# A two-layer trunk on one core: TensorE's order in layer 1 written out, with the scan's pieces set between dense steps

## The chip, the cores and the metric

The kernel runs on one core of a Trainium2 chip. That core has a matrix engine (TensorE, PE in the profile, with its weight loads shown apart as PEld), three engines for elementwise work (VectorE as DVE, ScalarE as ACT, GpSimd as POOL) and a queue for transfers (SyncE, SP). Each engine works through its own list of instructions in the order in which the built program holds them, and waits on semaphores for what others have to deliver. The metric is the time of one execution in device microseconds (us); lower is better.

## The reference

The computation is one inference step of a trunk with two layers on 640 tokens of width 1024: 128 prompt tokens and 512 sample tokens. Each layer normalises its input, applies a shift and a scale that come from a conditioning vector, runs one branch, and adds the branch's output times a gate to the residual `x`. Layer 0's branch is a convolution branch. Layer 1's branch, where nearly all of this change lies, is a two-directional state-space scan:

```python
u = h @ w_in
z, xbc, dt_raw = jnp.split(u, [SSD_INNER, SSD_INNER + XBC_DIM], axis=-1)
xbc = jax.nn.silu(depthwise_conv(xbc, w_conv, b_conv))      # 5 taps
xs, bm, cm = split(xbc)                                     # 2048, 4 x 128, 4 x 128
dt = softplus(dt_raw + bias);  a_cum = cumsum(dt * a)       # in chunks of 128 tokens
y_diag  = ((C B^T) * exp(segment sums)) @ (xs * dt)         # inside a chunk
state   = state * exp(a_cum[-1]) + B^T (decay * dt * xs)    # from chunk to chunk
y_off   = C @ state * exp(a_cum)
y = y_forward + flip(y_backward) + d_skip * xs
y = rms_norm_per_group(y * silu(z)) @ w_out
```

There are 4 groups of 8 heads; each group has its own B and C and its own normalisation. The kernel also returns the final scan states of the prompt.

## The kernel before

Tokens lie along the free axis and channels on the 128 partitions. All matrix products of the two layers are made in three passes of a split format: an operand is written as a rounded high part and a low part (`h_hi`, `h_lo`; `wh`, `wl`), and high x high, high x low and low x high are summed in PSUM. `split_w` (L73) loads one 128x1024 block of weights over the SP queue, has ACT round it to `wh` (L78), and has DVE or POOL subtract to get `wl` (L80). One output tile of 128 channels by 640 tokens takes 48 such matmuls (8 k-steps, 3 passes, 2 halves of the tokens). The profile counts all dense matmuls under the helper's line, L153, and the last output products under L1011. The dense tiles share one pair of PSUM buffers (`mm`), so that the tile after next waits until ACT or DVE has emptied the first.

In layer 1 each of the four groups g needs, as dense tiles: four tiles of x (`xs`), one of B, one of C, four of the gate (`pz`), and, once the group's y is normalised, eight products with `w_out` (`o2`; `out2`, four weight blocks with two tiles each). Between the dense tiles lie small matmuls in full precision, which are called pieces below:

- `ptx` (L757): transposes that turn a convolved x or B tile into token order (`to_tokens`);
- `pst` (L805): the state that one chunk adds; its operand `xw` is made by POOL (L803), and the carried state `stn` by POOL (L819) and DVE (L820);
- `pcb` (L855): C B^T of a chunk; DVE multiplies it into the decays `gf` (L864), which come from a transfer from DRAM (issued on ACT's queue), a subtraction on POOL (L841), a selection on DVE (L842) and an exponential on ACT (L848);
- `po` (L868): y_off for each direction; DVE scales it (L870) and POOL adds it to `y` (L871); `y` starts as a POOL product (L862);
- `py` (L876): y inside the chunk, 8 heads; ACT copies it to `yt` (L878);
- `pty` (L881): transposes of `y`; DVE adds them to `yt` (L882) and multiplies the sum into the gate `zs` (L889), chunk by chunk;
- `rms` (L921, L927): the sums and the spreading of a group's normalisation, with ACT's square root (L923) and DVE's reciprocal (L924) between them.

There are five chunks per group. What sets the order of all this: the program is written as generators (`phase_x`, `phase_bc`, `phase_z`, `phase_b`, `out2`), one after the other, and `phase_b` with the whole scan of a group runs under a raised priority (`tc.high_priority(offset=AHEAD)`, AHEAD 1000). The scheduler of the framework then merges them engine by engine by its own simulated times. Three `tc.issue_after` holds keep the exponentials behind the Silu of C and the square root of the group before (so that ACT changes its tables less often), and hold one gate tile back behind the normalisation.

## Time and profile before

| | |
|---|---|
| three runs | 1164.13, 1152.19 and 1165.15 us; median 1164.13 |
| the profiled execution | 1158.88 us, of which its span is 1157.1 us |
| granted TensorE clock, mean | 0.969 |
| busy: PE, PEld, DVE, ACT, POOL | 1084.6, 987.2, 819.0, 543.3, 563.9 us |
| layer 1 begins (first `dt` product) | 567.8 us; the first dense tile after the opening products starts at 591.1 us |

PE is the engine that is nearly always busy. A busy PE, however, is not a PE at its peak: the ends of matmuls are modelled, and the granted clock falls to half in some stretches. So PE's lost time has two parts, the idle time and the share of the clock that was not granted.

### The profile page before, as it was taken

Reading aid. Unit: us, or ns where it says so; the run is one execution under the profiler, and the core shown is the slowest. Engines: PE = TensorE matmul, PEld = TensorE weight load, DVE = VectorE, ACT = ScalarE, POOL = GpSimd, SP = SyncE. Lnnn points to the kernel's source line nnn. Section 1 sums busy time; section 2 is a strip of 40 time slices with the busy share of each in tenths; the row PEclk is TensorE's granted clock in tenths of the full one; section 3 lists DMA queues with packets and bytes.
Section 4 is the critical chain, followed back from the end, with each engine's and each line's share of the span. In section 5 each row is a group of like instructions: output and inputs, shape, how many; then the busy total and the mean of one; then the engine's idle time right before and its main releaser. Section 6 shows DMA issues by size and latency. Waiting matters only on the chain.

```text
span 1157.1 us, 18924 instructions
## 1 busy us (share of the span) xinstructions
PE 1084.6 (94%) x7532; PEld 987.2 (85%) x7532; DVE 819.0 (71%) x1170; ACT 543.3 (47%) x857; POOL 563.9 (49%) x475
## 2 busy tenths in 40 slices
PE   6999999999999999999999998979999998999996
PEld 3798879788899999999889977848899888998786
DVE  2478999899899599313768588745786278845875
ACT  6534456546554456212557655444165323753331
POOL 1155787869779448000000567567610766038410
PEclk8999999999999999999999999979999998999997
DMA  9334224323222211514231633414431344223302
GB/s 363 146 119 137 93 90 134 128 92 104 92 67 66 70 46 59 174 61 137 74 94 62 153 113 114 125 50 131 126 109 56 92 142 131 74 73 110 92 1 92
DMA packets 79048, 121.21 MB, mean 105 GB/s; under 512 B 5488, under 2 KB 49008, under 8 KB 78960
## 3 DMA queue, kind: packets, MB, share of 16 engines
q1 hardware_dynamic: 36720, 99.03, 25.9%
q10 hardware_dynamic: 42240, 20.98, 6.5%
q8 instruction: 59, 0.97, 0.3%
q14 instruction: 29, 0.24, 0.1%
HBM read 115.07 MB, written 4.92 MB: 104 GB/s over the span
## 4 chain that ended last, share of the span: by engine, by line
PE 67%; DVE 11%; ACT 6%; DMA 6%; POOL 5%; issue 4%; SPq 1%; ACTq 0%; DVEq 0%; POOLq 0%
PE xs L153 6%; PE o L153 6%; PE pz L153 5%; PE C L153 2%; PE B L153 2%; PE pst L805 2%; PE po L868 2%; ACT wh L78 2%; DMA wa<-w_ada 2%; DMA gf<-acd 2%; DVE cn L519 2%; DVE cva L356 2%; DMA gb<-acd 1%; PE o L1011 1%; PE o__5390 L144 1%
## 5 line engine op out<-in xcount | busy, mean ns | idle before, releaser
L356 DVE SCALAR_TENSOR_TENSOR cva<-v,cst,cva 128x550 f32<-128x550 f32 (+12 forms) x386 | 286.3, 815 | 9.2 <-ACT cva L349 7.7
L78 ACT CAST wh<-wf 128x1024 fp32r<-128x1024 f32 (+1 forms) x128 | 127.0, 993 | 251.0 <-PE o__4921 L144 37.6
L80 POOL TENSOR_TENSOR wl<-wf,wh 128x1024 fp32r<-128x1024 f32 (+1 forms) x62 | 148.2, 2390 | 128.4 <-ACT wh L78 123.5
L80 DVE TENSOR_TENSOR wl<-wf,wh 128x1024 fp32r<-128x1024 f32 (+1 forms) x66 | 79.9, 1210 | 91.3 <-ACT wh L78 91.1
L385 POOL TENSOR_TENSOR cv<-cv,tp 128x490 f32<-128x490 f32 (+3 forms) x94 | 113.4, 1210 | 13.4 <-ACT cv L383 9.0
L153 PE MATMUL o<-yhl,wh 128*128 128x320 f32 x384 | 93.3, 326 | 0.0
L841 POOL TENSOR_TENSOR gf<-gf,cols 128x512 f32<-128x512 f32 x40 | 46.2, 1164 | 81.7 <-DVE cols L728 63.9
L803 POOL TENSOR_TENSOR xw<-xt,cols 128x512 f32<-128x512 f32 x32 | 36.1, 1139 | 97.4 <-ACT xt L758 65.5
L153 PE MATMUL pz<-h_hi,wl 128*128 128x384 f32 (+1 forms) x256 | 83.4, 326 | 0.0
L380 ACT ACTIVATE tp<-v,cst 128x490 f32<-128x490 f32 (+3 forms) x94 | 65.9, 716 | 37.4 <-POOL cv L385 37.2
L153 PE MATMUL pz<-h_hi,wh 128*128 128x384 f32 (+1 forms) x256 | 82.0, 320 | 0.2 <-ACT zs L789 0.2
L153 PE MATMUL pz<-h_lo,wh 128*128 128x384 f32 (+1 forms) x256 | 81.8, 320 | 0.0
L153 PE MATMUL xs<-h_hi,wh 128*128 128x384 f32 (+1 forms) x224 | 72.8, 325 | 0.5 <-ACT up L641 0.5
L153 PE MATMUL xs<-h_hi,wl 128*128 128x384 f32 (+1 forms) x224 | 73.1, 327 | 0.0
L841 POOL TENSOR_TENSOR gb<-gb,cols 128x512 f32<-128x512 f32 x40 | 47.6, 1196 | 51.5 <-DMA gb<-acd 37.7
L736 DVE SCALAR_TENSOR_TENSOR xs<-up,cst,xs 128x642 f32<-128x642 f32 x64 | 68.5, 1077 | 4.8 <-ACT xs L734 4.0
L153 PEld LDWEIGHTS o<-yhl,wh 128*128 128x128 f32 x384 | 65.0, 189 | 7.6 <-issue 7.4
L153 PE MATMUL xs<-h_lo,wh 128*128 128x384 f32 (+1 forms) x224 | 71.5, 319 | 0.0
L842 DVE COPY_PREDICATED gf<-msk,gb 128x512 f32<-128x512 int32 x40 | 40.3, 1020 | 38.7 <-POOL gf L841 32.1
L153 PE MATMUL o<-yhl,wl 128*128 128x320 f32 x192 | 63.5, 331 | 0.0
L630 POOL MEMSET up<- 128x2 f32 x2 | 0.2, 100 | 117.2 <-DVE h_lo L215 117.2
L871 POOL TENSOR_TENSOR y<-y,yo 128x512 f32<-128x512 f32 x32 | 46.8, 1463 | 14.2 <-DVE yo L870 13.3
(681 smaller groups left out, 3364.9 us busy)
## 6 DMA issues: line engine op xcount, KB each, us to landing
wf<-w_in SPq DMA_DIRECT2D x48, 512.0 KB, 3.5
wa<-w_ada SPq DMA_DIRECT2D x64, 256.0 KB, 5.1
wf<-w_out SPq DMA_DIRECT2D x24, 512.0 KB, 3.5
wf<-w_xbc SPq DMA_DIRECT2D x24, 512.0 KB, 3.6
gf<-acd ACTq DMA_DIRECT2D x40, 256.0 KB, 4.0
gb<-acd ACTq DMA_DIRECT2D x40, 256.0 KB, 3.4
wa<-w_ada SPq DMA_DIRECT2D x16, 512.0 KB, 9.9
wf<-w_z SPq DMA_DIRECT2D x16, 512.0 KB, 3.6
```

The source lines that it names most:

```text
L78: S.copy(out=wh[:, :n], in_=wf[:, :n])
L80: sub.tensor_sub(out=wl[:, :n], in0=wf[:, :n], in1=wh[:, :n].bitcast(F32))
L153: T.matmul(ps[:, b, at : at + t1 - t0], lhsT=w, rhs=t[:, t0:t1], start=k == 0 and n == 0, stop=k == nk - 1 and n == 2)
L356: V.scalar_tensor_tensor(out=rows(acc)[:, :, lo:hi], in0=rows(v)[:, :, lo + d : hi + d], scalar=w_dw(i, tap), in1=rows(acc)[:, :, lo:hi], ...
L380: S.activation(out=tp[:, :, 0 : hi - lo], in_=rows(v)[:, :, lo + d : hi + d], func=AF.Copy, scale=w_dw(i, tap))
L385: G.tensor_add(out=rows(out)[:, :, lo:hi], in0=rows(out)[:, :, lo:hi], in1=tp[:, :, 0 : hi - lo])
L519: then(V.tensor_sub(out=t, in0=cv[i], in1=mu))
L736: V.scalar_tensor_tensor(out=acc, in0=u[:, d : d + PW], scalar=c("w_c", j * 5 + d), in1=acc, op0=ALU.mult, op1=ALU.add)
L803: G.tensor_mul(out=D8(xw), in0=D8(xt[ch]), in1=bc64(cols2[ch], 32 * back + o8))
L841: last_sub[g] = G.tensor_sub(out=gt, in0=gt, in1=cols1[ch][:, o : o + 4].unsqueeze(2).broadcast_to([P, 4, 128]))
L842: V.copy_predicated(out=gf, mask=msk.unsqueeze(1).broadcast_to([P, 4, 128]), data=gb)
L871: G.tensor_add(out=y, in0=y, in1=yo)
```

## The change

1. **A written-out order of TensorE in layer 1.** The generators are cut finer. The dense work becomes one list, `fill`, whose steps of six matmuls (`dense_steps`) come one after the other: x(0), B(0), C(0), x(1), z(0), B(1), C(1); then for g = 1 and 2 x(g+1), the products with `w_out` of group g-1, z(g), B(g+1), C(g+1); for g = 3 z(3) and the products of group 2; then the last products. A planner, `drive`, keeps a clock that each matmul advances by a fixed amount, and between two dense steps it sets a piece as soon as the piece's planned time has come and what it needs has been set. The scan of group g gives each of its steps a distance in shares of a period (7.5, 17, 17 and 9.5 us for the four groups), transposes come 13 us after their tile, and the normalisations have distances of 3 to 6 us. At the end every PE instruction of layer 1 is tied to the one before it, so the scheduler can't change PE's order; the other engines' order is still the scheduler's, with a raised priority (AHEAD 300) for scan, normalisation and transposes.
2. **y in x's place.** ACT copies `py` over the chunk's x (`xt`), and DVE adds `pty` there. `yt` is gone.
3. **The gate follows the last chunk.** z is computed between the chunks; its product with y is made when all chunks of the group are done (8 products per half of the tokens, of 64 and 256 columns, in place of one of 512 per chunk). `yh` and `yl` are made in halves.
4. **Holds gone, queues changed.** The `issue_after` holds are gone. The saved states are loaded over ACT's queue, no longer over SP's. The `wl` of the first groups' x, B and C tiles are subtracted on POOL instead of DVE.
5. **Start of layer 0.** The first two blocks of the conditioning product get two more 128x256 products after each fourth matmul (8 in all), into a PSUM tile that is overwritten later.

The core of the diff:

```diff
+            if busy is not None and k % 4 == 3:
+                for b in range(2):
+                    T.matmul(busy[:, b, 0:256], lhsT=w[:, 0:128], rhs=w, start=True, stop=True)
...
+        def drive(filler, streams):
+            needs = next(filler, None)
+            while True:
+                streams[:] = [z for z in streams if z.alive]
+                hit = [z for z in streams if z.free() and z.due <= clock[0]]
+                if hit:
+                    hit[0].step()
+                    continue
+                hit = [i for i, p in enumerate(pending) if p[0] <= clock[0]]
+                if hit:
+                    emit_pending(hit[0])
+                    continue
+                if needs is not None and all(n in done for n in needs):
+                    needs = next(filler, None)
+                    continue
...
+                clock[0] = max(clock[0], min(due))
...
+                        T.matmul(ps[:, b, at_ : at_ + t1 - t0], lhsT=w, rhs=t_[:, t0:t1], start=k == 0 and n == 0, stop=k == nk - 1 and n == 2)
+                        clock[0] += (t1 - t0) / 2400 + 0.0135
+                    if k % 2:
+                        yield ()
...
-                nc.sync.dma_start(out=st[c0], in_=a[key][g])
+                nc.scalar.dma_start(out=st[c0], in_=a[key][g])
...
-                            hold.enter_context(tc.issue_after(grp[g]["silu"].ins))
-                            if g:
-                                hold.enter_context(tc.issue_after(last_root[g - 1].ins))
...
             for n, ch in enumerate(order):
+                gfs = grp[g]["gfs"]
+                if n < 3:
+                    chain(n, 1)
+                if n < 4:
+                    grp[g]["gfs"] = decays(g, order[n + 1])
+                elif g < 3:
+                    grp[g + 1]["gfs"] = decays(g + 1, (ORDER if g < 2 else ORDER3)[0])
+                if n:
+                    yield 0.1 * T_, ()
+                    turn_y(order[n - 1], y)
+                yield 0.1 * T_, ()
...
-                yt = lp.tile([P, 512], F32, tag="yo", bufs=2, name="yt")
-                S.copy(out=yt, in_=py)
+                S.copy(out=xt[ch], in_=py)
+                yield (0.35 if n < 4 else 0.0) * T_, ()
...
+        def norm(g, sides):
+            yield 0.0, [("y", g, ch) for ch in chs] + ([("out2", g - 1, mp) for mp in range(4)] if g else [])
+            for j in range(4):
+                yield 0.0, [("z", g, j)]
...
+                        V.tensor_mul(out=z, in0=z, in1=yv)
+            done.add(("gated", g))
...
+        drive(filler(), [Stream(scans()), Stream(norms()), Stream(final(1)), Stream(final(0))])
+        for ins in nc.cur_bb.bb.instructions[begun:]:
+            if ins.engine == mybir.EngineType.PE:
+                if prev is not None:
+                    tc.add_manual_dep(ins, prev, mybir.DependencyInfo(mybir.DependencyClass.NoSync, mybir.DependencyReason.DATA), reason="order")
+                prev = ins.name
```

Three places show what this does to the order. The first is PE at the normalisation of group 0. Before, the end of the gate tiles is followed by both halves of the sums, their spreading and five states at a stretch, with no dense step among them (`pz` is a dense step of the gate, `ptx` a transpose of B, `pst` a state):

```order
L153 MATMUL pz<-h_hi,wl 128x256
L921 MATMUL rms<-ysq,ones 32x160 x8
L757 MATMUL ptx<-cst,B 128x128
L921 MATMUL rms<-ysq,ones 32x160 x8
L927 MATMUL rms<-rq,cst 128x160 x4
L805 MATMUL pst<-xw,Bt 128x512 x5
L153 MATMUL pz<-h_hi,wh 128x384
```

Now the sums of group 0 come in four parts among the x tiles of group 2; after the first of them stand 18 dense matmuls, of which the first three are shown, then the second part:

```order
L809 MATMUL xs<-h_hi,wl 128x384
L1067 MATMUL rms<-ysq,ones 32x160 x4
L809 MATMUL xs<-h_hi,wh 128x384
L809 MATMUL xs<-h_lo,wh 128x384
L809 MATMUL xs<-h_hi,wl 128x384
```

The sums, the spreading and the states have each moved apart, with 6 to 24 dense matmuls between two of them.

The second place is PE at the end of group 3, from the last dense step of group 2's products with `w_out` (`o_10740`) to the first of the last products (`o_10913`), as it stands now:

```order
L809 MATMUL o_10740<-yhl,wl 128x320
L1067 MATMUL rms<-ysq,ones 32x160 x2
L972 MATMUL pty<-cst,y 128x128 x4
L991 MATMUL pcb<-C,B 128x128
L1007 MATMUL po<-st_f_10071,C 128x512
L1067 MATMUL rms<-ysq,ones 32x160 x2
L1007 MATMUL po<-stn,C 128x512
L1022 MATMUL py<-gf,xt 64x128 x8
L1067 MATMUL rms<-ysq,ones 32x160 x4
L972 MATMUL pty<-cst,y 128x128 x4
L1077 MATMUL rms<-rq,cst 128x160 x2
L1152 MATMUL o_10913<-yhl,wh 128x320 x2
```

Between the last `o_10740` and the first `o_10913` no dense step is left: the whole last chunk and the normalisation of the second half of the tokens lie there. Before, the last chunk's pieces began among dense steps of the same products (`o_10410`):

```order
L855 MATMUL pcb<-C,B 128x128
L153 MATMUL o_10410<-yhl,wh 128x320 x2
L868 MATMUL po<-st_f_10464,C 128x512
L153 MATMUL o_10410<-yhl,wl 128x320
L153 MATMUL o_10410<-yhl,wh 128x320 x2
L153 MATMUL o_10410<-yhl,wl 128x320
L153 MATMUL o_10410<-yhl,wh 128x320 x2
L927 MATMUL rms<-rq,cst 128x160 x2
L153 MATMUL o_10410<-yhl,wl 128x320
L153 MATMUL o_10410<-yhl,wh 128x320
L868 MATMUL po<-stn,C 128x512
```

They went on so through the next tile (`py` behind 14 of its matmuls), and that chunk's `pty` stood 47 matmuls into the last products. The dense work that used to cover the last chunk has been moved ahead of it.

The third place is ACT in the scan of group 0, now, around the exponentials of a chunk's decays (`gf`), with Silu of an x tile before them (`up` is where the next dense tile is emptied to, `wh` the rounded weights):

```order
L827 ACT_TABLE_LOAD
L827 ACTIVATE xs<-xs 128x642
L916 ACT_TABLE_LOAD
L916 ACTIVATE gf<-gf 128x512
L911 DMA gb<-acd 128x4x128
L78 CAST wh<-wf 128x1024
L916 ACTIVATE gf<-gf 128x512
L911 DMA gb<-acd 128x4x128
L638 COPY up_5967<-xs 128x128
L639 COPY up_5967<-xs 128x512
```

Before, in the scan of group 1, the exponentials of two chunks followed on one load (`yt` is the copy of `py`):

```order
L848 ACT_TABLE_LOAD
L848 ACTIVATE gf<-gf 128x512
L840 DMA gb<-acd 128x4x128
L78 CAST wh<-wf 128x1024
L848 ACTIVATE gf<-gf 128x512
L840 DMA gb<-acd 128x4x128
L840 DMA gf<-acd 128x4x128
L878 COPY yt<-py 128x512
L840 DMA gf<-acd 128x4x128
L78 CAST wh<-wf 128x1024
L848 ACTIVATE gf<-gf 128x512
```

Silu of the x tiles, which changes the table, has come between the exponentials. In layer 1 the list of ACT held 33 table loads before (13 at the exponentials, 10 at the convolved tiles, 6 at the gate, 4 at the square roots); it now holds 44 (18, 11, 11 and 4).

499 lines of the change are left out of this document (305 added, 194 removed).

## Prediction

> **What bounds the kernel now.** I read the page first: of 1157.1 us PE is idle for 72.5, no other engine is busy for more than 71%.
>
> ```profile
> span 1157.1 us, 18924 instructions
> PE 1084.6 (94%) x7532; PEld 987.2 (85%) x7532; DVE 819.0 (71%) x1170; ACT 543.3 (47%) x857; POOL 563.9 (49%) x475
> ```
>
> The change sits in layer 1, so next I cut that layer into stages (the view of windows; columns: stage, its length, busy us of PE, PEld, DVE, ACT, POOL, then the granted clock and the transfers). The stages are: the opening and group 0's scan; group 0's normalisation and group 1's scan; the dense stretch and group 2's scan; its normalisation with the dense tiles behind it; group 3's scan; the end.
>
> ```profile
> 590.00:735.00 145.00, 134.73 (x873) 122.98 (x871) 113.43 (x146) 83.90 (x130) 67.45 (x51) 0.98 0.38 112
> 735.00:835.00 100.00, 89.36 (x563) 74.32 (x563) 63.60 (x97) 37.65 (x57) 66.25 (x51) 0.93 0.36 108
> 835.00:960.00 125.00, 123.75 (x844) 112.67 (x843) 79.15 (x117) 55.51 (x90) 54.45 (x45) 1.00 0.34 103
> 960.00:1030.00 70.00, 66.90 (x481) 65.05 (x480) 53.53 (x64) 39.00 (x65) 21.28 (x16) 0.95 0.31 92
> 1030.00:1100.00 70.00, 68.26 (x431) 56.31 (x430) 43.09 (x71) 24.39 (x41) 44.70 (x35) 0.98 0.30 91
> 1100.00:1157.00 57.00, 45.51 (x290) 41.21 (x289) 37.68 (x88) 14.65 (x33) 3.62 (x3) 0.86 0.13 47
> ```
>
> What PE loses in a stage is its idle time plus the clock not granted (length times one minus the clock). In order that is 10.3+2.9, 10.6+7.0, 1.3+0, 3.1+3.5, 1.7+1.4 and 11.5+8.0 us: 13.2, 17.6, 1.3, 6.6, 3.1 and 19.5, together 61.3. An order can win nothing else in layer 1, since the number of its matmuls does not change. The 41.8 us before 1100 are the ceiling for the pieces; the end has its own reasons.
>
> Then who PE waits for (the view of waits, PE alone, from 590 us on; us in total, times, longest):
>
> ```profile
> PE pty L881 <- POOL y L871: 5.3, 3, 2.6
> PE pst L805 <- POOL xw L803: 5.3, 4, 3.5
> PE pty L881 <- POOL y L862: 3.9, 2, 3.1
> PE ptx L757 <- ACT xs L737: 3.1, 1, 3.1
> PE rms L927 <- DVE rq L924: 2.6, 1, 2.6
> ...
> PE xs L153 <- ACT up L641: 0.5, 1, 0.5
> ```
>
> All are pieces that stood in PE's list before their operand was made; no dense tile waits for its weights, and only one for a buffer, 0.5 us. The second stage shows how such waits come on top of one another (windows again):
>
> ```profile
> 755.00:760.00 5.00, 2.64 (x9) 2.63 (x10) 2.32 (x4) 4.58 (x7) 4.74 (x4) 0.50 0.34 105
> 760.00:765.00 5.00, 3.76 (x6) 0.92 (x4) 5.00 (x10) 2.60 (x4) 2.78 (x2) 0.81 0.00 0
> 765.00:770.00 5.00, 2.19 (x4) 0.80 (x4) 2.11 (x4) 1.46 (x2) 5.00 (x5) 0.87 0.01 2
> 770.00:775.00 5.00, 4.78 (x14) 3.77 (x13) 0.62 (x1) 2.31 (x6) 2.42 (x3) 0.50 0.27 102
> ```
>
> Here PE runs only 33 matmuls in 20 us, is idle for 6.6, and the clock is at half for the first and last five.
>
> **The change part by part.** Prices of a dense tile of 48 and of two pieces (the chain in order of time: start, us, what):
>
> ```profile
> 777.10 0.86 PE pst L805 x2
> 783.79 1.02 PE py L876 x16
> 1002.64 7.03 PE B L153 x48
> ```
>
> So a dense matmul costs 0.147 us, and a state 0.86.
>
> *Group 0's normalisation and group 1's start.* Their pieces now stand among x tiles with 6 to 24 dense matmuls, 0.9 to 3.5 us, between two. The chain sums, root, reciprocal, spreading has 24 dense matmuls and two states (5.2 us) between sums and spreading; the wait for `rq` was 2.6 us with nothing between, so it is covered. The states waited up to 3.5 us for `xw`; now 12 or more dense matmuls lie between them. Of 17.6 us I leave 5: DVE also convolves x tiles here, and half of the longest waits may remain. Gain 12.6 (bounds 5 and 17.6).
>
> *Group 2's normalisation* is the same move with smaller waits: of 6.6 I leave 3, a gain of 3.6 (bounds 0 and 6.6).
>
> *Group 0's scan.* Here POOL must be weighed against PE, for z and x(1) are now all that fills it. POOL's operations (the view of groups from 590 us on: count, busy us, mean ns, then its idle time):
>
> ```profile
> L841 POOL TENSOR_TENSOR gb<-gb,cols 128x512 f32<-128x512 f32 x40 | 47.6, 1196 | 51.5 <-DMA gb<-acd 37.7 <-DVE gf L864 7.1 <-DVE xs L736 6.6
> L871 POOL TENSOR_TENSOR y<-y,yo 128x512 f32<-128x512 f32 x32 | 46.8, 1463 | 14.2 <-DVE yo L870 13.3
> L841 POOL TENSOR_TENSOR gf<-gf,cols 128x512 f32<-128x512 f32 x40 | 46.2, 1164 | 81.7 <-DVE cols L728 63.9 <-DMA gf<-acd 12.8 <-DVE C L736 2.3
> L803 POOL TENSOR_TENSOR xw<-xt,cols 128x512 f32<-128x512 f32 x32 | 36.1, 1139 | 97.4 <-ACT xt L758 65.5 <-PE pst L805 31.8
> L862 POOL TENSOR_TENSOR y<-xt,co 128x512 f32<-128x512 f32 x20 | 26.3, 1315 | 11.0 <-DVE wl L999 9.5 <-DVE co L860 1.5
> L819 POOL TENSOR_TENSOR stn<-stn,decb 128x512 f32<-128x512 f32 x16 | 19.8, 1237 | 5.4 <-DVE stn L820 5.4
> ```
>
> A chunk costs POOL two `gf` and two `gb` (4.7), `y` (1.3) and two additions (2.9): 9.0; a state step adds 2.4 (`xw`, `stn`), a final prompt state 1.1. That is 12.5 for the first two chunks, 11.3 for the third, 9.0 for the fourth. By the new order PE has, from one `pty` to the next, 60 dense matmuls and pieces (14.5 us), 54 (11.3), 24 (7.0) and 72 (12.3). POOL is ahead at first, level at the second gap, and 2 us late at the third; PE waits there, and at the first `xw`, which needs four subtractions and itself (5.9 us) after the columns, where PE has 24 dense matmuls (3.5): 2.4. The wait for `ptx` (3.1) stays, since that piece stands no later than before, and some 2.5 for `py` where DVE still selects decays ahead of it. Sum 10 of 13.2, a gain of 3. Bounds: the whole 13.2, or a loss of 12 if POOL keeps the pace of before (first rival).
>
> *The end of the dense list.* Nothing dense covers group 3's last chunk any more. After the last `o_10740` the chain is: C B^T, DVE's work on it, POOL's `y` and two additions (1.3+2.9), DVE's share between, transposes, and beside it root, table load, reciprocal, spreading and the first `yh`: by these prices and the delays in group 0 about 12 us, with 6 us of pieces to run. PE idles for some 6; this is new. Loss 6.5 with a slice of the clock (bounds 2 and 12).
>
> *The last stage* keeps its shape: the second half's products wait for sums and root, and a final stretch of output and transfers.
>
> ```profile
> 1124.00:1128.00 4.00, 4.00 (x13) 3.10 (x14) 2.98 (x8) 2.20 (x6) 0.00 (x0) 0.50 0.00 0
> 1128.00:1132.00 4.00, 2.81 (x10) 2.41 (x10) 4.00 (x11) 0.00 (x0) 0.00 (x0) 0.50 0.70 246
> ```
>
> Between 1124 and 1132 the first half's six scalings on DVE stand before the second half's normalisation; the planner spaces them out. I count 4 (bounds 0 and 8).
>
> *Start of layer 0.* The clock there is at half while transfers run at their full rate:
>
> ```profile
> 20.00:22.00 2.00, 1.24 (x12) 0.67 (x12) 0.86 (x2) 1.32 (x2) 0.67 (x1) 0.79 1.03 409
> 22.00:24.00 2.00, 2.00 (x15) 1.53 (x7) 0.00 (x0) 0.00 (x0) 1.69 (x1) 0.50 1.04 411
> 30.00:32.00 2.00, 2.00 (x14) 1.19 (x14) 2.00 (x2) 0.64 (x1) 1.56 (x1) 0.65 1.04 414
> ```
>
> Half clock from 21 to 31 us costs 5. The eight extra products lie in front of this stretch, where PE is idle, and can keep the clock up; but transfers feed PE there, and the new order sets a matmul of the third tile sooner than its weights come. I take a gain of 2 (bounds 5, and a loss of 2 if the extra products delay the first normalisation). The Trainium skill, "TensorE: Matmul & The Clock Gate", Part 1, says that the clock returns to full after about 3.4 us of activity; by it the whole 5 would be won, and the sum be 3 lower.
>
> *Costs beside the path.* DVE's 8 smaller gate products, the halves of `yl` and ACT's halves of `yh` add about 2 us each per engine and lie on engines that are busy for 390 and 255 of 567 us. Moving 8 `wl` from DVE to POOL falls before the scan, where POOL is idle. The saved states' loads leave SP's queue, which frees weights behind them, and no dense tile waited for weights. ACT gets 11 more table loads (the view of groups):
>
> ```profile
> L848 ACT ACTIVATE gf<-gf 128x512 f32<-128x512 f32 x40 | 24.3, 628 | 49.5 <-DVE gf L842 47.8 <-DMA gb<-acd 1.6
> L848 ACT ACT_TABLE_LOAD x13 | 16.7, 1283 | 0.2
> ```
>
> At 1.283 us that is 14.1 us on an engine that has 312 free; I count nothing, but it is the root of the third rival.
>
> **The sum.** 12.6 + 3.6 + 3 - 6.5 + 4 + 2 = 18.7 us less than the profiled execution's own 1158.88: 1140. That execution lies 5.2 under the median of the runs shown (1164.13) and 6.7 over the fastest (1152.19), so a median may come out some 5 us to either side.
>
> **The rivals.** *First: nothing is won, since the scan has a pace of its own.* Transposes of `y` before, four of group 0 and the first two of group 1 (PE in order of time):
>
> ```profile
> 686.13 0.60 PE L881 MATMUL pty<-cst,y 128*128 128x128 f32 x4
> 702.63 0.66 PE L881 MATMUL pty<-cst,y 128*128 128x128 f32 x4 [2.64 <-POOL y L871]
> 719.10 0.65 PE L881 MATMUL pty<-cst,y 128*128 128x128 f32 x4 [1.86 <-POOL y L871]
> 730.83 0.66 PE L881 MATMUL pty<-cst,y 128*128 128x128 f32 x4
> ...
> 788.16 0.60 PE L881 MATMUL pty<-cst,y 128*128 128x128 f32 x4
> 802.86 0.60 PE L881 MATMUL pty<-cst,y 128*128 128x128 f32 x4
> ```
>
> Those of group 0 came 16.5, 16.5 and 11.7 us apart. If that is what transfer, POOL, DVE and ACT need in a row for a chunk, not what the old order left them, PE waits 2.0, 5.2 and 4.7 us against the new 14.5, 11.3 and 7.0: 12 us in group 0. Group 3, which is planned nearly as tight, would add 6. The gain of 18.7 falls to 1: 1158, between 1150 and 1168. For it: POOL's 37.7 us of idle time on `gb` transfers, which the sum of busy times leaves out. Against it: group 1's first chunk took 14.7 us with the same work.
>
> *Second: the pieces are never late.* Then of the 41.8 us only the wait for `ptx` stays (3.1), the gap at the end shrinks to 2, and with 4 and 2 from the ends the gain is 42: 1117, between 1108 and 1128. For it: from 835 to 960, where dense steps and pieces were already mixed, PE lost 1.3 in 125 us. Against it: POOL's count for group 0.
>
> *Third: slower, because ACT is held.* The exponentials now stand on ACT among the copies that empty the dense tiles (`up`) and the roundings of weights (`wh`). An exponential waits for DVE's selection: 49.5 us over 20 chunks, 2.4 each. With a load to its table and one back, a chunk holds ACT for 5 us. PE has one buffer in reserve, a dense tile of 7.03 us, so the hold is hidden as long as it stays under that. It decides as soon as DVE comes to the selection late by four of the convolution's operations (some 4 us): then PE waits 2.3 to 3 us per chunk, 46 to 60 us over 20 chunks. From 1140 that is 1186 to 1200, with half of the chunks some 1168. For it: the holds that kept exponentials behind Silu are gone. Against it: no dense tile waited before for more than 0.5 us on ACT, though ACT then waited 47.8 us at the same place. The Trainium skill, "ScalarE: Activation LUTs", What ACT_TABLE_LOAD costs and the section on table sets, speaks against this change: it gives 1.28 us for the load and as much again for a drain, 2.66 us a switch, and says to finish with one set before going to the next. The row agrees on the load, and no row here shows the drain; by it the hold would be an estimated 7.7 us and this rival would decide without DVE's being late.
>
> **How the numbers follow.** The forecast has a chance of 0.50, with a range of its own from 1128 to 1150; the first rival 0.17, the second 0.22, the third 0.11. A measurement of this kernel can tell about 2% from no change; on the profiled execution's time that line is at 1136. A bit under half of the forecast's chance (0.22) and the second rival lie below it: faster 0.44. The rest of the forecast (0.28) and the first rival lie within: 0.45. Slower: 0.11. The range of 1113 to 1170 leaves out the lower part of the second rival (0.06) and nearly all of the third.
>
> **What the changed profile would show.** Right: in the stage of group 0's normalisation PE's idle time falls from 10.6 to a few us, and the clock there goes from 0.93 to about 1; the waits for `rq` and `xw` all but go; a gap of 4 to 8 us appears ahead of the first of the last products, after which the clock dips; `pty` of group 0 comes 12 to 15 us apart at first. First rival: long waits of `pty` for `y` in groups 0 and 3. Second: less than 5 us of waits before that gap. Third: dense tiles that wait for ACT's `up` or `zs`. The forecast is wrong if the gap at the end costs over 12 us, if the first state waits long for columns that come later than before, or if layer 0 moves by more than 5 us, which I have not looked for beyond its first 60.

## The result, and the profile after

The changed kernel takes 1201.51 us (median, 1199.82 to 1205.28) where the kernel before takes 1158.16 (1150.32 to 1165.15): a ratio of 1.038, with a 95% interval from 1.029 to 1.047. It is slower; the forecast was 1140. The page of the changed kernel, its span and its busy times:

```profile
span 1198.0 us, 19044 instructions
PE 1090.4 (91%) x7548; PEld 988.6 (83%) x7548; DVE 844.6 (71%) x1218; ACT 561.7 (47%) x880; POOL 589.0 (49%) x483
```

Apart from the extra products at the start PE does the same work, and it is idle for 107.6 us instead of 72.5. Nearly all of the difference lies in layer 1, which I count from the first matmul of `dt` (PE in order of time, the kernel before and the changed one):

```profile
567.80 0.90 PE L144 MATMUL dt<-h_hi,wh 128*128 128x384 f32 x2 [0.55 <-ACT h_hi L210]
```

```profile
565.63 0.56 PE L148 MATMUL dt<-h_hi,wh 128*128 128x384 f32 x2 [0.55 <-ACT h_hi L214]
```

From there to the end of the span is 589.3 us before and 632.4 after: 43.1 more. To see where, I cut both kernels at the same events: first dense tile, first state of group 0, then the last `py` of group 0, 1, 2 and 3, and the end. (Windows; columns as in the prediction: stage, length, busy us of PE, PEld, DVE, ACT, POOL, granted clock, transfers.) Before:

```profile
590.80:657.10 66.30, 62.35 (x421) 61.47 (x421) 52.03 (x71) 43.26 (x69) 10.04 (x9) 0.97 0.40 111
657.10:738.50 81.40, 75.33 (x475) 64.59 (x475) 64.53 (x81) 40.77 (x61) 58.66 (x45) 0.98 0.38 116
738.50:837.60 99.10, 88.10 (x551) 72.90 (x551) 62.70 (x97) 37.78 (x57) 66.63 (x52) 0.93 0.36 107
837.60:973.60 136.00, 135.11 (x928) 123.73 (x928) 86.61 (x127) 58.72 (x95) 62.05 (x51) 1.00 0.35 105
973.60:1101.10 127.50, 122.65 (x819) 109.26 (x818) 87.65 (x122) 60.10 (x99) 56.74 (x44) 0.96 0.28 87
1101.10:1157.10 56.00, 44.41 (x283) 40.30 (x282) 36.58 (x86) 13.68 (x31) 3.62 (x3) 0.85 0.14 48
```

The changed kernel, at the same events:

```profile
588.60:657.50 68.90, 55.02 (x349) 53.20 (x349) 60.41 (x68) 40.19 (x65) 32.55 (x17) 0.94 0.36 103
657.50:739.20 81.70, 70.89 (x425) 59.77 (x426) 56.05 (x78) 38.77 (x56) 56.90 (x44) 0.92 0.37 109
739.20:884.70 145.50, 134.84 (x886) 120.79 (x885) 95.28 (x135) 65.61 (x102) 69.69 (x53) 0.96 0.31 93
884.70:1027.20 142.50, 133.59 (x880) 118.88 (x879) 92.50 (x138) 66.34 (x102) 66.03 (x51) 0.98 0.32 97
1027.20:1132.90 105.70, 97.39 (x652) 83.31 (x652) 71.33 (x123) 45.57 (x72) 53.51 (x42) 0.98 0.30 90
1132.90:1198.00 65.10, 46.32 (x280) 40.97 (x280) 37.26 (x89) 16.76 (x37) 3.03 (x3) 0.80 0.12 41
```

The lengths of a stage cannot be compared, since the dense work in it differs. What can be compared is the loss as the prediction counts it, idle time plus length times one minus the clock:

| stage | loss before | loss after | difference |
|---|---|---|---|
| opening, to the first state | 5.9 | 18.0 | +12.1 |
| scan of group 0 | 7.7 | 17.3 | +9.6 |
| normalisation of group 0, scan of group 1 | 17.9 | 16.5 | -1.4 |
| normalisation of group 1, scan of group 2 | 0.9 | 11.8 | +10.9 |
| normalisation of group 2, scan of group 3 | 10.0 | 10.4 | +0.4 |
| from group 3's last `py` to the end | 20.0 | 31.8 | +11.8 |

The sum of the differences is 43.4, the whole of the 43.1. Four rows stand out: the opening, group 0's scan, the stretch around group 1's normalisation, which had lost almost nothing before, and the end. A single stage, however, moves from one execution to the next: the run without the extra products (under "The other two parts"), whose layer 1 is written the same, takes 634.0 us for it and loses 21.8, 16.2, 11.5, 11.2, 14.0 and 32.1 us in these six stages. Differences of up to 5 us in one stage are therefore no evidence by themselves.

PE's waits in the changed kernel, first from 588 to 740 us (us in total, times, longest):

```profile
PE ptx L846 <- ACT xt L848: 8.6, 5, 3.7
PE pty L972 <- POOL y L1011: 6.6, 1, 6.6
PE pst L940 <- POOL xw L938: 5.6, 1, 5.6
...
PE xs L809 <- POOL wl L80: 1.2, 1, 1.2
```

From 740 to 1133, and from 1133 to the end:

```profile
PE rms L1067 <- ACT ysq L1059: 11.4, 6, 3.2
PE o L809 <- DVE x L168: 3.5, 2, 2.6
```

```profile
PE o L1152 <- ACT yhl L1086: 4.4, 2, 2.7
PE o L1152 <- DVE yhl L1087: 2.2, 2, 1.6
```

Added up over all of layer 1, the waits that this view labels are 65.8 us; in the kernel before they are 32.2. They are called labelled waits below. The waits for `rq` and most of those for `xw` in the normalisations went, as forecast, and waits of the sums (`rms`) for the squares took their place: before, these had been 2.2 us in all. At the end, the second half waits for its normalised rows. DVE there (in order of time), the kernel before and the changed one:

```profile
1125.32 1.92 DVE L932 SCALAR_TENSOR_TENSOR zs<-zs,cst,rms 128x320 f32<-128x320 f32 x4 [0.77 <-PE rms L927]
1127.16 0.48 DVE L934 TENSOR_TENSOR yhl<-zs,yhl 128x320 fp32r<-128x320 f32 x1
1127.56 2.83 DVE L1031 SCALAR_TENSOR_TENSOR fo<-x,cst,rps 128x320 f32<-128x320 f32 x6
```

```profile
1165.18 2.84 DVE L1190 SCALAR_TENSOR_TENSOR fo<-x,cst,rps 128x320 f32<-128x320 f32 x6 [1.20 <-PE rps L182]
1167.94 1.92 DVE L1085 SCALAR_TENSOR_TENSOR zs<-zs,cst,rms 128x320 f32<-128x320 f32 x4
```

Before, the scaling of the second half's rows (`zs`) stood ahead of the six output scalings of the first half (`fo`). Now the six stand ahead of it: PE spreads the normalisation (`rms`) only from 1164.94 us on, after the products that the output scalings wait for.

### The profile page after: what moved, and what is told of

Its sections match the earlier page's. It is cut to its first block, busy times and chain, and to the rows that moved or that the text cites. A ratio compares the mean times of both kernels' runs of the same rounds, so it can differ in the third digit from the quotient of the medians.

```text
span 1198.0 us, 19044 instructions
## 1 busy us (share of the span) xinstructions
PE 1090.4 (91%) x7548; PEld 988.6 (83%) x7548; DVE 844.6 (71%) x1218; ACT 561.7 (47%) x880; POOL 589.0 (49%) x483
## 5 line engine op out<-in xcount | busy, mean ns | idle before, releaser
L80 POOL TENSOR_TENSOR wl<-wf,wh 128x1024 fp32r<-128x1024 f32 (+1 forms) x70 | 170.0, 2430 | 160.9 <-ACT wh L78 148.6
L80 DVE TENSOR_TENSOR wl<-wf,wh 128x1024 fp32r<-128x1024 f32 (+1 forms) x58 | 73.0, 1259 | 94.8 <-ACT wh L78 94.6
L826 DVE SCALAR_TENSOR_TENSOR xs<-up,cst,xs 128x642 f32<-128x642 f32 x64 | 83.5, 1310 | 12.8 <-ACT xs L824 12.2
L809 PE MATMUL pz<-h_hi,wh 128*128 128x384 f32 (+1 forms) x256 | 89.4, 349 | 0.0
L809 PE MATMUL xs<-h_hi,wh 128*128 128x384 f32 (+1 forms) x224 | 81.2, 363 | 0.5 <-ACT up L639 0.5
L913 DVE COPY_PREDICATED gf<-msk,gb 128x512 f32<-128x512 int32 x40 | 42.8, 1094 | 54.1 <-POOL gf L912 52.7
L809 PE MATMUL pz<-h_hi,wl 128*128 128x384 f32 (+1 forms) x256 | 79.6, 311 | 0.0
L809 PE MATMUL o<-yhl,wl 128*128 128x320 f32 x192 | 59.7, 311 | 0.0
L938 POOL TENSOR_TENSOR xw<-xt,cols 128x512 f32<-128x512 f32 x32 | 39.6, 1240 | 40.7 <-PE rms L1067 33.4
L809 PEld LDWEIGHTS pz<-h_hi,wh 128*128 128x128 f32 x256 | 48.9, 191 | 7.0 <-issue 7.0
```

Of the source, the lines that this page charges most:

```text
L80: sub.tensor_sub(out=wl[:, :n], in0=wf[:, :n], in1=wh[:, :n].bitcast(F32))
L809: T.matmul(ps[:, b, at_ : at_ + t1 - t0], lhsT=w, rhs=t_[:, t0:t1], start=k == 0 and n == 0, stop=k == nk - 1 and n == 2)
L826: V.scalar_tensor_tensor(out=acc, in0=u[:, d : d + PW], scalar=c("w_c", j * 5 + d), in1=acc, op0=ALU.mult, op1=ALU.add)
L913: V.copy_predicated(out=gf, mask=msk.unsqueeze(1).broadcast_to([P, 4, 128]), data=gb)
L938: G.tensor_mul(out=D8(xw), in0=D8(xt[ch]), in1=bc64(cols2[ch], 32 * back + o8))
```

## The experiments

Layer 0 is the same code in nearly all these kernels, and yet layer 1 began anywhere from 564.6 to 572.8 us. So beside the time each verdict gives the length of layer 1, from the first `dt` to the end of the span, against 632.4 of the changed kernel and 589.3 of the kernel before. These are mostly single profiled executions; I take nothing under about 4 us for a difference.

### The tie of TensorE's order

```diff
-        for ins in nc.cur_bb.bb.instructions[begun:]:
-            if ins.engine == mybir.EngineType.PE:
-                if prev is not None:
...
-                prev = ins.name
```

> The changed kernel without the last loop, which ties each TensorE instruction of layer 1 to the one before it; everything is still emitted in the planned sequence, but the scheduler sets TensorE's order. Theory A (the written order sets pieces ahead of operands that come later than the plan's delays; 33 us more of labelled waits, and about 10 us of clock behind them): the waits fall back towards 32 us and the time to 1160-1175. Theory B (ACT is held by the exponentials' table loads, so that copies come late whatever the order): 1190-1205, with the same waits for ACT.

Measured: 1177.0 us, layer 1 605.2, so 27.2 of the 43.1 come back. By the same six events the losses are 11.7, 16.4, 10.1, 10.6, 8.7 and 15.2, together 72.7 against 62.4 in the kernel before; so 5.6 of the 15.9 us that layer 1 is still longer stand in no stage's loss, but in PE's busy time. The last stage, where it shows most (windows):

```profile
1115.30:1175.20 59.90, 49.48 (x337) 45.21 (x336) 41.13 (x97) 18.95 (x40) 1.15 (x1) 0.92 0.16 53
```

Its loss of 15.2 stands against 31.8; the opening gains 6.3 and group 0's normalisation 6.4. The scan of group 0 still loses 16.4 and the opening 11.7, so these parts have a cause beside the tie. Theory A (the written order puts pieces where their operands are not ready) holds for the larger part of the loss; labelled waits fell to 48 us only, not to 32.

### The exponentials on ACT

```diff
-            for gf in gfs:
-                S.activation(out=gf, in_=gf, func=AF.Exp)
```

> The changed kernel without the 40 exponentials of the decays (the decays are left as the selected differences, so the scan's result is another one). It takes 25 us of exponentials and about 20 table loads, 25 us, off ACT. Theory B (ACT held): waits for xt, xs, ysq, up and yhl, 31 us of the 65, fall by more than half and the time to 1165-1180. Theory A (the plan's delays): the time stays within 1188-1203, since only the py waits for gf (2.2 us) and a share of the xt waits go.

The kernel leaves out the exponentials, so its result is another one. Measured: 1195.4, layer 1 626.8: 5.6 us less. The table loads of layer 1 fall from 47 to 12 and ACT loses 25 us of exponentials, and yet the long waits remain (`pty` for `y` 6.7, `pst` for `xw` 3.5, `ptx` for the convolved tiles). Theory B, my third rival, falls: what ACT holds is hidden nearly everywhere.

### The pace of group 0, and POOL's list

```diff
-            for g, T_ in enumerate((7.5, 17.0, 17.0, 9.5)):
+            for g, T_ in enumerate((10.0, 17.0, 17.0, 9.5)):
```

> The changed kernel with the pace of group 0's scan set from 7.5 to 10. Theory A: between two transposes of y lie some 40% more dense matmuls, the 6.6 us wait for y in group 0 goes, the first wait for xw (5.6) and the ptx waits (9) stay: 1188-1194. Theory C (POOL's list in a row has its own pace, about 15 us a chunk): the same gain here, 5 to 9 us. If instead the lost time is only moved on, to the dense tiles that wait for group 0's normalisation, it stays at 1196-1203.

Measured: 1206.1, layer 1 636.4: 4.0 more. The wait of 6.6 for `y` became 1.3 and 3.8, one of 2.7 for `gf` and one of 4.9 for `xt` came, and the dense list ran out, so that group 0's third to fifth `py` stand after 98 to 102 us of dense matmuls, nearly on top of one another. Both theories had this wrong; only the alternative that the lost time is moved on is left standing.

```diff
                 if n < 3:
                     chain(n, 1)
-                if n < 4:
-                    grp[g]["gfs"] = decays(g, order[n + 1])
...
+                if n < 4:
+                    grp[g]["gfs"] = decays(g, order[n + 1])
                 if n == 4:
                     done.add(("scan", g))
```

> The changed kernel with the decays of the next chunk emitted after this chunk's y and its two additions instead of ahead of them, so that POOL's subtractions on gb, which wait for transfers (43.9 us of POOL's idle time), no longer stand before y. Theory C: the 6.6 us wait of pty for y in group 0 goes and those at the end (1.5 and 1.0) fall: 1186-1193. Theory A without C: the decays only come later, py waits for gf instead (more than the 2.2 us it has now): 1198-1215.

Measured: 1209.6, layer 1 635.0: 2.6 more, and `pty` still waits 5.9 for `y`. POOL's subtractions ahead of `y` were not what held it; theory C falls.

### The stock of dense work beside group 0

```diff
+        def bc_tile(g):
+            us = []
+            for name in ("B", "C"):
...
+                yield from dense_steps(ps, wh, wl, h, [k * 128 for k in range(KD)], ODD)
+                us.append(evacuate(ps))
...
+            if g:
+                yield (("scan", g - 1),)
```

> The changed kernel in which the B and C tiles of the next group run their dense matmuls (two tiles of 7.03 us) before the plan waits for the end of the running scan, and only their convolutions wait. Theory D (group 0's scan keeps its pace in real time, and what the new order changed is the stock of dense work beside it: the last py of group 0 stands after 101 us of dense matmuls, against 119 before): that py now stands after 109, so 8 us come back, 1187-1193. Theory A (single delays of the plan are too short, the stock does not matter): the waits only move, 1196-1203.

Measured: 1200.1, layer 1 631.3. Group 0's last `py` indeed stands after 109 us of dense matmuls, but it also starts 181.6 us after the start of layer 1 instead of 173.6: eight more done, eight more taken. Theory D in this form falls. Time since the start of layer 1 less 0.147 us for each dense matmul that stands ahead in the list, the time lost by that point, is some 72.6 in both (about 51.7 in the kernel before).

### The delays before the sums, and at the end

```diff
-                yield 3.0, ()
+                yield ((7.0 if j == 0 else 4.0) if g < 3 else 3.0), ()
                 if j == 0:
                     ps[sides[0]] = spare("rms")
```

> The changed kernel with the plan's delays between the squares of a group's normalisation and their sums set from 3 to 7 for the first and to 4 for the others, in groups 0 to 2. Theory E (the gate products of a whole group now stand in a row between the last chunk and the first square, a chain that the delay of 3 does not cover): the six waits of rms for ysq in groups 0 to 2, 11.4 us, and the half clock that comes behind each go, 1184-1193. Rival: what is blocked until the normalisation is done comes later by the same, 1196-1205.

Measured: 1194.9, layer 1 622.8, 9.6 us less; layer 1 had begun 4.8 us later than in the changed kernel, which hides half of it in the time. The third and fourth stage (windows) and the wait of the sums up to 1133 us:

```profile
744.20:880.40 136.20, 131.38 (x888) 117.29 (x889) 89.53 (x135) 65.13 (x102) 73.34 (x53) 1.00 0.33 99
880.40:1018.60 138.20, 131.05 (x879) 117.69 (x879) 92.55 (x138) 68.80 (x104) 68.00 (x51) 0.99 0.34 100
```

```profile
PE rms L1067 <- ACT ysq L1059: 3.2, 4, 1.2
```

The same matmuls take 9.3 and 4.3 us less there, idle time and clock alike: losses of 4.8 and 8.5 against 16.5 and 11.8, and the waits are 3.2 instead of 11.4. Theory E holds: a delay of 3 was too short for sixteen gate products and a square. Of the 13.6 us in these two stages 9.6 are left in layer 1, since the opening and the end lose more than in the changed kernel.

```diff
-                yield 3.0, ()
+                yield (3.0 if g < 3 else 1.5), ()
...
-                yield (6.0 if b == sides[0] else 4.0), ()
+                yield ((6.0 if g < 3 else 3.0) if b == sides[0] else 4.0), ()
```

> The changed kernel with the plan's delays of group 3's two normalisations halved (3 to 1.5 between squares and sums, 6 to 3 before the spreading). Theory F (the second half's normalisation is spread over the whole of the first half's products by these delays, so that its scaling falls behind the first half's six output scalings on DVE): the waits for yhl at the second half, 2.7 and 1.6 us, and the half clock behind go, 1191-1195. Rival: the sums wait for the squares on the spot and nothing is won, 1197-1203.

Measured: 1197.6, layer 1 629.1, which no single execution tells from no change. The stage from group 3's last `py` to the end is 59.6 us and not 65.1, and it loses 25.1 instead of 31.8; 4.7 of this gain is clock. DVE has the scaling of the second half's rows ahead of the six output scalings again, as before the change, and yet the waits for `yhl` are 5.6 instead of 6.6: they were not what shortened it, so the mechanism that I gave is not shown.

The three edits in one kernel:

> The edits of the three runs before in one kernel. If they are separate causes the gains add: 8 + 10 + 6, 1174-1182. If they are one slack that is spent once, it is no better than the best of them, 1185-1193.

Measured: 1188.3, layer 1 615.4: 17.0 us less, a little over the sum of the single gains (1.1 + 9.6 + 3.3). The expectation missed since it had 8 for the early tiles.

### Where the opening loses

```diff
-                later(42.0 + n, lambda n=n, z=z: turn_columns(n, z))
-            later(49.0, lambda: None, ("cols",))
+                later(50.0 + n, lambda n=n, z=z: turn_columns(n, z))
+            later(59.0, lambda: None, ("cols",))
```

> The changed kernel with the pieces that turn the time steps' columns set 8 and their readiness 10 later in the plan, so that the first state of group 0 stands after 70 us of dense matmuls (as before) and not after 60; but the dense work that may run beside group 0's scan ends as before the edit, so its last py still stands after 101 (119 before). Read from the start of layer 1, to leave layer 0 out. Theory D (what counts is how much dense work may stand beside the scan until its end): the first state comes with no wait, and the time lost is only moved to the later chunks, within 3 us of the changed kernel. Theory A (a piece set too early is the loss by itself): the 5.6 us for xw and part of the ptx waits are won, 6 to 10 us less.

Measured: 1200.8, layer 1 634.3: no difference. The first state came 11.3 us later, with 9.7 us more dense matmuls ahead of it. So it is not pinned to a time at which its operand is ready: counted in the same way, PE loses some 32 to 34 us up to it wherever it stands (about 19 in the kernel before). So it is not this delay alone; something else slows the opening too.

All edits together, and transposes of x tiles later:

```diff
-        TURN = 13.0
+        TURN = 16.0
...
-            later(TURN + 2.0, lambda: part(0, 1), key)
+            later(TURN + 5.0, lambda: part(0, 1), key)
```

> All at once: columns later, B and C dense tiles early, longer delays before the sums in groups 0 to 2, shorter ones in group 3, and the transposes of x tiles 3 later (13 to 16, the second 5 behind the first instead of 2). The last py of group 0 now stands after 113 us of dense matmuls. Theory D: group 0's scan ends at the same real time with 12 us more work done, 10 us less than the kernel with three edits (1188.3), so 1174-1181. If the scan is only pushed out by what stands beside it, as with the B and C edit alone: 1185-1192.

Measured: 1197.2, layer 1 624.4, worse than three of its edits. Where these 9.0 us went is not shown: the opening loses about as much as with the three edits (18.8 and 18.2), and the scan and the normalisation of group 0 and the end lose more. But one new wait in the opening points to DVE (waits of PE, 594 to 673 us):

```profile
PE ptx L846 <- ACT xs L827: 8.7, 1, 8.7
```

The transposes now wait for the convolved tile itself, which ACT finishes from DVE's steps. Two parts of the change load DVE there. The four x tiles of group 1 stand where z tiles stood, and each brings four convolution steps; and the eight subtractions `wl` that went to POOL run beside DVE's work. DVE's convolution steps and one small operation in the opening, the kernel before and the changed one (groups; count, busy us, mean ns):

```profile
L736 DVE SCALAR_TENSOR_TENSOR xs<-up,cst,xs 128x642 f32<-128x642 f32 x16 | 13.8, 883 | 2.8 <-ACT xs L734 2.8
...
L682 DVE SCALAR_TENSOR_TENSOR e<-xr 128x384 f32<-128x384 f32 x1 | 0.6, 561 | 0.0
```

```profile
L826 DVE SCALAR_TENSOR_TENSOR xs<-up,cst,xs 128x642 f32<-128x642 f32 x22 | 27.2, 1253 | 2.5 <-ACT xs L824 2.4
...
L680 DVE SCALAR_TENSOR_TENSOR e<-xr 128x384 f32<-128x384 f32 x1 | 2.5, 2518 | 0.0
```

More of them, and each longer. Why that one operation takes 2.52 us shows beside POOL (both engines of the changed kernel in order of time):

```profile
588.37 4.71 POOL L80 TENSOR_TENSOR wl<-wf,wh 128x1024 fp32r<-128x1024 f32 x2 [7.41 <-ACT wh L78]
```

```profile
590.98 2.52 DVE L680 SCALAR_TENSOR_TENSOR e<-xr 128x384 f32<-128x384 f32 x1
```

POOL's second subtraction ends at 593.08; DVE's operation, 0.56 us long when alone, ends at 593.50. It has been held until POOL was done. The twenty-two convolution steps are not all longer by the same: sixteen last 0.87 to 0.92 us, as before, three that run while POOL makes a `wl` last 2.9 to 3.0, and three later ones, beside POOL's work on the decays and on `xw`, about 1.5. Each of the two parts was undone by itself:

```diff
-            item(x_tile(0, j), a["w_xbc"][j] if j > 1 else None, G)
+            item(x_tile(0, j), a["w_xbc"][j] if j > 1 else None)
...
-            item(x_tile(1, j), a["w_xbc"][4 + j], G)
+            item(x_tile(1, j), a["w_xbc"][4 + j])
```

> The changed kernel with the eight subtractions wl of the first tiles back on DVE. Theory H (each of POOL's 2.4 us subtractions holds the DVE operation that runs beside it: 0.88 us for a convolution step alone, 1.63 beside POOL): DVE gains more in the opening than its own subtractions (1.3 us each) cost, the first state comes 2 to 6 us sooner after the start of layer 1 (91.9 now), and layer 1 is 2 to 6 us shorter than 632.4. Rival (moving them off DVE is worth its own time): DVE carries 9 us more in the opening and the first state comes 3 to 9 us later.

Measured: 1196.3, layer 1 629.3, 3.1 less. The convolution steps are back at 969 ns, but DVE's own nine subtractions take 12.2 us there, and the first state comes at 93.0 us instead of 91.9. The two nearly cancel. The opening (windows) loses 20.8 us where it lost 18.0:

```profile
588.20:658.20 70.00, 56.21 (x349) 54.38 (x349) 57.92 (x76) 41.39 (x66) 11.78 (x9) 0.90 0.34 102
```

```diff
-        for j in range(4):
-            item(x_tile(1, j), a["w_xbc"][4 + j], G)
         for g in range(NG):
...
             for j in range(4):
                 item(z_tile(g, j), a["w_z"][4 * g + j])
+            if g == 0:
+                for j in range(4):
+                    item(x_tile(1, j), a["w_xbc"][4 + j], G)
```

> The changed kernel with the four z tiles of group 0 set ahead of the four x tiles of group 1 in the dense list, as before. Theory G (x tiles in the opening bring four convolution steps each to DVE, which is busy for 85 to 92% there, so that the transposes and the first state wait): the waits up to the first state fall from 13.5 us to 5 or less, and the first state comes 6 to 10 us sooner; as the stock beside the scan is no larger, up to half of it is lost again by the scan's end: layer 1 is 5 to 10 us shorter than 632.4. If DVE is not what holds it: no change, 628-636.

Measured: 1200.7, layer 1 628.7, 3.7 less; the first state came 1.1 us sooner only. By itself this is not enough either, and the opening loses 17.7 us:

```profile
593.20:661.00 67.80, 55.56 (x349) 53.57 (x349) 50.96 (x65) 37.90 (x62) 19.68 (x13) 0.92 0.33 97
```

To see POOL's subtractions alone, the kernel before was given that one part:

```diff
-            wh, wl = split_w(src, 1024, V)
+            nin[0] += 1
+            wh, wl = split_w(src, 1024, G if nin[0] <= 8 else V)
```

> The kernel before with one part of the change alone: the wl subtractions of its first eight tiles of layer 1 that are split there (x 2 and 3, B, C, z) on POOL. Theory H: each holds the DVE operation beside it, convolution steps there last over 1.2 us and not 0.88, and the first state comes 2 to 6 us later than 89.3 us after the start of layer 1. Rival (DVE is relieved by 8 x 1.3 us and POOL was idle): 0 to 5 us sooner.

Measured: 1174.5, layer 1 602.9 against 589.3: 13.6 us longer. Its opening (windows), its convolution steps there (groups) and the waits of PE there:

```profile
592.80:663.30 70.50, 59.39 (x376) 58.03 (x377) 55.15 (x63) 42.24 (x65) 34.12 (x19) 0.93 0.36 103
```

```profile
L739 DVE SCALAR_TENSOR_TENSOR xs<-up,cst,xs 128x642 f32<-128x642 f32 x16 | 22.2, 1405 | 0.0
```

```profile
PE pt L727 <- DVE t L718: 3.5, 1, 3.5
PE ptx L760 <- ACT xs L740: 2.8, 1, 2.8
PE pt L727 <- DVE v L714: 2.6, 1, 2.6
PE xs L153 <- POOL wl L80: 1.2, 1, 1.2
```

The same sixteen steps take 22.2 us instead of 13.8: twelve last at most 0.88 us and four, beside a `wl` on POOL, 2.99 to 3.03. The time steps' columns, which are a chain on DVE, come late, and the opening loses 16.0 us instead of 5.9. Theory H holds there. DVE is rid of nine of its ten subtractions in this stage and is yet busy for 55.2 us and not 52.0: moving them to the idle engine gives the busy one no relief, and what is held stands in the chain to the first state. Some of the 13.6 lies further on (a z tile waits 6.4 us for ACT), which I have not followed up.

### All together, with and without the tie

The written order kept, with z before x(1), `wl` on DVE, early B and C tiles, later columns and the changed delays (edits as above):

> The written order kept, with z before x(1), the wl subtractions on DVE, B and C dense tiles early, columns 8 to 10 later, and the changed delays of the sums. The first state stands after 70 us of dense matmuls and group 0's last py after 113. If theories D, G and H hold together, group 0 ends with some 55 us lost and not 72.6 (51.7 before), and layer 1 takes 595-608: 1163-1176. If the written order costs by itself whatever its numbers, 612 or more.

Measured: 1182.8, layer 1 614.7: the opening is right, the whole is not. Its first stage (windows) and its longest waits:

```profile
589.30:656.20 66.90, 62.87 (x422) 61.33 (x422) 52.29 (x71) 39.81 (x66) 10.75 (x9) 0.97 0.38 113
```

```profile
PE ptx L846 <- ACT B L827: 11.7, 1, 11.7
PE py L1026 <- DVE gf L1005: 9.3, 4, 5.7
PE pst L944 <- POOL xw L942: 8.9, 5, 5.5
```

The opening loses 6.0 us, as the kernel before does (5.9), and by group 0's last `py` 56.4 us are lost, where 55 were expected. So it took these parts together to bring the opening back; none of them undone alone did, and how they share the loss is not shown. Then one piece alone, the transposes of group 1's B, stands 11.7 us too early, and the stage in which it lies loses 27.7 us where the changed kernel lost 16.5. New waits came for those that went: the nine tied kernels with an edited plan took back 17.7 us at most and stayed between 614.7 and 636.4.

The same without the late columns and without the tie:

> The same without the late columns and without the tie of TensorE's instructions. Without the tie alone layer 1 took 605.2, all of its 16 us over the kernel before in group 0. Theory G and H: these 16 fall to 5 or less, layer 1 takes 588-596, 1156-1165, the time of the kernel before. If group 0's loss has another cause: 600-606.

Measured: 1166.3, layer 1 599.0: 33.4 of the 43.1 are back. 9.7 remain, where 5 or less were expected. The opening (windows) is not what came back against the kernel that is only untied:

```profile
588.50:652.80 64.30, 57.88 (x366) 56.58 (x366) 52.17 (x70) 40.23 (x64) 10.76 (x8) 0.92 0.37 105
```

It loses 11.6 us, where that one lost 11.7, though the subtractions are on DVE and z stands ahead of x(1).

The dense list of this one put in the sequence of the kernel before in all groups:

> The free version of the last run (no tie, z before x(1), wl on DVE, B and C early, changed delays of the sums), with the dense list in the sequence of the kernel before in all groups: B, C, z of the group, the products of the group before, then the next group's x tiles. Layer 1 took 599.0 there, 589.3 in the kernel before. Theory J (x tiles ahead of z cost in every group, since they bring convolutions to DVE beside the scan): 588-594 now, no difference to the kernel before that can be measured. If what is left comes from the plan's other parts: 597-602, slower by about 1%.

Measured: 1173.9 (1170.0 to 1174.7) against 1158.2, a ratio of 1.013 with an interval from 1.010 to 1.016; layer 1 607.7. Theory J falls: this sequence is not what is left, and the later groups ran no better for it.

### The other two parts

The kernel before with `y` in x's place and the gate products at the start of the normalisation:

```diff
-                S.copy(out=yt, in_=py)
+                S.copy(out=xt[ch], in_=py)
...
             def normalised(sides):
+                for j in range(4):
+                    for b in sides:
...
+                            V.tensor_mul(out=z, in0=z, in1=yv)
```

> The kernel before with one part of the change: y is put in x's place and the gate products stand at the start of the normalisation (16 small ones in groups 0 to 2) and not behind each chunk; TensorE's order stays the scheduler's. Theory E (the longer chain from last chunk to squares costs time where nothing dense covers it): 3 to 8 us in the three normalisations and at the end, 1162-1170. Rival: the scheduler fills the place with dense work, 1154-1162, and the chain only hurts where the order is written out.

Measured: 1161.2 against 1162.2, layer 1 592.0 (589.3): no difference that can be told in the whole. By the six events the stage of group 0's normalisation loses 24.8 us instead of 17.9, and the last two lose 4.7 and 14.3 instead of 10.0 and 20.0; whether the chain costs there and something else gains, or the stages vary, one execution does not tell. In the written order, longer delays for the same chain were worth 9.6 us.

```diff
-            ada_block(*ada_load(0, k, wat, 4), sps.tile([P, 512], F32, tag="ada", bufs=2, name="ada"), u0 if k < 2 else None)
+            ada_block(*ada_load(0, k, wat, 4), sps.tile([P, 512], F32, tag="ada", bufs=2, name="ada"), None)
```

> The changed kernel without the eight extra products at the start of layer 0. If they keep the clock up, the granted clock between 20 and 40 us falls from 1.00 to about 0.74 and layer 1 begins 2 to 4 us later than in the other runs of this order (565.6 to 572.8): 1200-1206. If they do nothing that lasts, layer 1 begins in the same span and the time is 1195-1203.

Measured: 1202.6. The stretch from 20 to 40 us, without the extra products and with them (windows):

```profile
20.00:40.00 20.00, 18.44 (x123) 12.76 (x124) 9.36 (x14) 10.51 (x20) 4.71 (x2) 0.83 0.93 371
```

```profile
20.00:40.00 20.00, 18.18 (x151) 13.59 (x151) 9.08 (x13) 11.35 (x22) 4.79 (x2) 1.00 0.92 366
```

They do hold the clock. But layer 1 begins at 566.8 without them, and from 564.6 to 572.8 with them: nothing of it can be told by then. With them PE waits 2.8 us for ACT at 350.9 us, a wait that the kernel without them does not have.

## Why the prediction was wrong, point by point

**The sum as a whole.** It took what each stage lost before as all that was at stake ("An order can win nothing else in layer 1"), and priced new waits only in group 0's scan and at the end. This is the step that failed: a piece that the plan sets ahead of its operand stops the whole engine, and outside these two places such stops were put at nothing. Labelled waits doubled, from 32.2 to 65.8 us. With the tie alone taken out they are 47.5, and layer 1 is 27.2 us shorter: the largest part of the 43.1.

**Group 0's normalisation and group 1's start, a gain of 12.6.** That stage gained 1.4 (6.4 in the second execution of the same layer 1). The waits that I wanted gone are gone; the step that failed is the one before: I let the chain begin with the sums. Its inputs come from sixteen gate products that now follow the last chunk, and the plan gave them a delay of 3. With 7 and 4 the stage loses 4.8, which is 13.1 less than before, near the 12.6 of the forecast; layer 1 is 9.6 shorter. The move was right, the delay was mis-sized. **Group 2's normalisation, a gain of 3.6**, gave -0.4. The longest wait for a square, 3.2 us, is there; with the longer delays it is 1.2 at most, but a wait of 3.7 for `gf` came and the stage loses 10.7, so the delay is not the whole reason.

**The dense stretch, no term.** I read its loss of about 1 us as nothing to win and gave it no price. It lost 10.9 more. An order can win no more than what is lost before, as I wrote, but it can lose anywhere: the sentence has only one side, and the sum inherited that.

**Group 0's scan, a gain of 3, at worst a loss of 12.** Opening and scan together lost 21.7 more, outside both bounds. Of the four waits in the sum, which made 10 us, three came where they were set and were larger: `pty` for POOL's `y` at the third gap, 2 in the forecast, took 6.6; the first `xw`, 2.4, took 5.6; `ptx`, 3.1, took 9.2 in all; that of `py` (2.5) did not come. The wait for `xw` is close to a sign that the prediction had named, a long wait of the first state for its columns. What was put at nothing is the step under "costs beside the path": the eight subtractions were not counted since POOL is idle there. POOL was; DVE, which they hold, was busy for 52 of 66 us. Moved alone, in the kernel before, they raise the loss of the opening from 5.9 to 16.0 (one execution). The x tiles in z's place were not priced on DVE in this stage, only on PE. With both undone, the columns later and B and C early, the opening was as before. Each undone alone left its loss where it was (20.8 and 17.7), so which of them carries how much of the 12.1 is open.

**The end, a loss of 6.5 and a gain of 4.** The gap came (windows):

```profile
1133.00:1145.00 12.00, 7.07 (x42) 5.18 (x43) 7.78 (x16) 5.49 (x10) 2.93 (x3) 0.69 0.00 0
```

It costs 4.9 us of idle time and 3.7 of clock, within the bounds of 2 and 12. Without these 8.6 the stage lost 23.2 where it lost 20.0 before, so the term with the wrong sign is the gain of 4. The prediction read the last stage of the kernel before the wrong way round: the six output scalings did not stand before the second half's normalisation but behind its four scalings (the rows above). Now they do stand before it, since the plan spread the sums of the second half over the first half's products.

**The start of layer 0, a gain of 2.** The clock behaved as described (1.00 with the extra products, 0.83 without them, 0.74 in the kernel before). The Trainium skill, "TensorE: Matmul & The Clock Gate", Part 1, ties the clock to activity in this way, and the rows agree. The time at the start of layer 1 shows nothing of it.

**ACT's table loads at nothing.** Nearly right: 35 loads and all exponentials are worth 5.6 us in layer 1, in one execution.

**The rivals.** The third came nearest with its figures (1168 to 1200), by luck: its reason does not hold, since the exponentials and table loads can be left out without the time coming back. The Trainium skill, "ScalarE: Activation LUTs", What ACT_TABLE_LOAD costs, spoke for it with the price of a switch; that price is not contradicted, but nearly all of it is hidden here. The first rival (the scan's own pace, POOL ahead of `y`) had one of its waits, 6.6 us, but group 0's transposes of `y` came 17.3, 13.6 and 13.0 us apart and not 16.5, 16.5 and 11.7, and neither a slower pace nor a POOL list with `y` ahead of the subtractions shortened layer 1. The second had the smallest share of truth: pieces are late at every normalisation. No rival was "the order is tied, and its numbers do not fit", though the tie alone is 27.2 of the 43.1 us.

**What stays open.** In the untied kernel with the edits 9.7 us of layer 1 are left. By the count of idle time and clock it loses 63.0 us in the six stages, the kernel before 62.4, so that count does not see what is left. Over layer 1 idle time is 7.6 us more, as are the labelled waits (`ptx` and `po` above all), and some 6 us more of the clock are granted; but PE's busy time is 2.1 us longer all the same. The matmuls and transposes of the x tiles are busy for 151.8 us there and for 140.9 before. Why, and which part of the change makes it, no run here tells; the holds, the queue of the saved states and the lower priority were not undone one by one.

## What to carry to other kernels

A written-out order of one engine turns each misjudged delay into a stall of the whole engine, so price what a stage without losses could lose, and first compare the tied program with the same program left to the scheduler. Before work goes to an idle engine, look at what runs beside it on the others, and follow a moved tile to every engine it feeds, not to the matmuls alone. When each edit of a plan brings new waits for those it removes, stop tuning it.

## What the runs showed of the hardware

POOL's subtraction of two tiles in SBUF holds a DVE operation that starts beside it until it ends: 2.52 us instead of 0.56, and some 3.0 us instead of 0.88 for four of sixteen convolution steps (1405 ns on the mean instead of 883). The Trainium skill, "SBUF — State Buffer", section "Who interferes with whom", says that a DVE instruction with two inputs in SBUF contends with a GpSimd instruction that reads SBUF, and calls the shared pair of ports an exclusive lock. These rows agree; the prediction had not drawn on it.

Eight extra products at the start kept the granted clock at 1.00 from 20 to 40 us, where it is 0.74 to 0.83 without them, and 530 us later nothing of that could be measured.
